# Turned tiles copied from SBUF to SBUF in sixteen pieces, and a DRAM tile of a triangular inverse stored by diagonal blocks

## The chip, the cores and the metric

The kernel runs on one core of one Trainium2 chip. The metric is the device time of one launch in microseconds (us), lower is better. Three runs of the kernel before took 2254.8, 2255.21 and 2257.08 us, so its median is 2255.21 us. One more execution was recorded with the hardware profiler, and every number of a trace in this text comes from it.

## The reference, cut to what matters

The program is one inference step of a decoder with two layers, for a prompt of 1024 tokens and a group of 8 samples of one token each. Both groups go through the same weights; the kernel keeps them side by side as 1032 columns. Each layer projects its normalised input with one large matrix, runs two kinds of recurrent heads, gates the result and projects it back:

```python
h = _rms(x, norm_w[layer]) * (1.0 + scale) + shift
proj = (h @ w_in).astype(f32)          # q, k, v, gates, z of all heads
...                                    # recurrent heads, per layer two kinds
x = x + gate * ((y * silu(z)) @ w_out)
```

The even layer has 8 gated-delta heads and 8 mLSTM heads, the odd layer 4 GLA heads and 4 retention heads. The recurrences are computed in chunks of tokens. Two pieces of this matter here. First, every head needs some of its operands (keys, values) with tokens on the rows, while the projections deliver them with features on the rows; so whole tiles have to be turned. Second, a gated-delta head solves a unit lower triangular system per chunk:

```python
A = jnp.where(tri_strict, decay * kk, 0.0) * beta_h[..., :, None]
rhs = beta_h[..., None] * (jnp.moveaxis(vc, 1, 2) - gam * jnp.einsum('bthd,bhde->bhte', kc, S))
U = lax.linalg.triangular_solve(A + eye, rhs, left_side=True, lower=True, unit_diagonal=True)
```

## The kernel before, in words

**Layout.** Activations lie with features on the 128 partitions and 1032 columns: 1024 prompt tokens and 8 samples. Chunks are 128 tokens long, so there are 8 of them (`NC`). A projection of 128 features is 72 matmuls of 128x128 by 128x344: three column ranges, eight blocks of the contraction, and three products each, since fp32 operands are split into a high and a low part (`whi`, `wlo` for the weights). The weights of one projection are one load of 512 KB into one of two `wf` tiles (`load_w`, L886).

**The order of the work.** No instruction is issued as the Python code reaches it. A class `Recorder` (L178) notes each operation with the memory it reads and writes (`touch`, L244), the operations that it therefore depends on, and an estimated cost, and then orders all of them by list scheduling (`forward`, `backward`), each engine's queue for itself. All DMA transfers are issued by one queue, SP. A transfer counts there as 360 ns of SP, a time that depends on its bytes and on the length of its contiguous runs, and a landing latency of 1400 ns, or 2100 ns above 256 KB. For a tile in SBUF the noted region is a range of partitions and a range of columns; for a tile in DRAM it is one range of addresses, from the first to the last that the access touches (`region`, L198). The engines then run the queues strictly in that order, with semaphores for the real dependences. Since PE's order is fixed too, PE stands still when its next matmul is not ready, even when a later one is.

**The even layer** (`even`, L2186) runs the eight gated-delta heads one after the other (`gdn_proj`, `gdn_mix`) and steps the mLSTM heads between them (`MSTEPS`, L35), so that their projections fill PE while a gated-delta head waits on its own chain. The chain of one gated-delta head is: keys from the convolution, turned and squared (`squares`, `kd`), the matrices `N` of all eight chunks, their inverse `Y` (`inverse`), eight chunk steps with the state `S`, and the output. The large tiles of a head (`k2`, `kd`, `N`, `EM`, `Y` and more) exist once, so that the next head waits for most of them. **The odd layer** (L2209) has the same shape with `gla_mix` and `ret_mix`.

**Turning a tile** (`squares`, L1697). VectorE can transpose 32x32 squares in place of their position. One instruction of it (L1702) turns all squares of the 128x1024 tile and writes them into `y` so that the four squares that belong to one destination partition range lie in one column range. What is left is to carry each 32x256 block from partition group `a`, column group `b` of `y` to partition group `b`, column group `a` of `z`. The kernel before does this through DRAM: one transfer of 512 KB writes `y` to one of four tiles `td` (L1705), and four transfers of 128 KB read it back, one for each group of 32 partitions (L1707). `squares` is called for the keys and values of each gated-delta head (L1199, L1210), for each pair of mLSTM heads (`kwe`, L1426), for the values and the output of each mLSTM head (L1467, L1530) and for the two halves of the values of each GLA and retention head (`v_tokens`, L1715).

**The inverse** (`inverse`, L1279). The 8 matrices of 128x128 have 32 diagonal blocks of 32x32, and each of these two diagonal blocks of 16x16. The 64 small blocks are gathered so that each lies on one partition: four transfers write the 32x32 blocks, one for each position `j` on the diagonal, into a DRAM tile `nd` of 64x528 (L1293), and one transfer reads the 16x16 blocks out of it (L1294). VectorE inverts them in 30 small instructions, the result goes to `yd` in the same way (L1300) and comes back in four reads (L1303). Larger blocks follow with matmuls. Row `m` of `nd` belongs to chunk `c`, position `j` and half `q` as `m = (c, j, q)`, the chunk outermost (L1284).

Of the kernel before, what the change touches and what calls it, by code (L numbers as in the profile page):

```python
# [9 lines left out]
F32 = mybir.dt.float32  # L10
# [7 lines left out]
T = 1024  # L18
# [6 lines left out]
NC = T // L  # L25
# [438 lines left out]
class Step:  # L464
# [814 lines left out]
    def inverse(self, N):  # L1279

        V, G, dma = self.nc.vector, self.nc.gpsimd, self.nc.sync.dma_start

        nd, yd = (self.nyd[x][self.turn(x, 2)] for x in ("nd", "yd"))
        by32 = lambda x, j: x.rearrange("(c j q) x -> c j (q x)", c=NC, j=4)[:, j, 0:1024].rearrange(  # L1284
            "c (s t) -> s c t", t=32)
        by16 = lambda x: x[:, 0:512].rearrange("m (r t) -> m r t", t=32)[:, :, 0:16]
        blocks = [slice(32 * j, 32 * j + 32) for j in range(4)]
        t = self.slot("EM", name="inv")
        D, At, qt, Dt = (t[:, 256 * i:256 * i + 256].rearrange("p (c t) -> p c t", c=NC) for i in range(4))
        nb, yb, tb = (t[0:64, 256 * i:256 * i + 256].rearrange("p (r t) -> p r t", t=16) for i in (1, 2, 3))  # L1290
        dma(yb, self.a["i16"].rearrange("p (r t) -> p r t", t=16))
        for j, b in enumerate(blocks):
            dma(by32(nd, j), N[b, :, b])  # L1293
        dma(nb, by16(nd))  # L1294
        for s in range(15):
            n = 15 - s
            V.tensor_tensor(tb[:, 0:s + 1, 0:n], yb[:, 0:s + 1, s:s + 1].to_broadcast([64, s + 1, n]),
                            nb[:, s:s + 1, s + 1:16].to_broadcast([64, s + 1, n]), op=ALU.mult)
            V.tensor_tensor(yb[:, 0:s + 1, s + 1:16], yb[:, 0:s + 1, s + 1:16], tb[:, 0:s + 1, 0:n], op=ALU.subtract)
        dma(by16(yd), yb)  # L1300

        for j, b in enumerate(blocks):
            dma(D[b], by32(yd, j))  # L1303
        V.transpose(Dt, D)
        p = self.ps(None, [128, NC, 32])
        for c in range(NC):
            for j, b in enumerate(blocks):
                self.mm(p[b, c, :], N[b, c, b], Dt[b, c, :], tile_position=(32 * j, 32 * j))
        V.tensor_tensor(At, p, self.imask.unsqueeze(1).to_broadcast([128, NC, 32]), op=ALU.mult)
        p = self.ps(None, [128, NC, 32])  # L1310
        for c in range(NC):
            for j, b in enumerate(blocks):
                self.mm(p[b, c, :], At[b, c, :], D[b, c, :], tile_position=(32 * j, 32 * j))
        V.tensor_tensor(D, D, p, op=ALU.subtract)
        V.transpose(Dt, D)
        Y = self.slot("Y", [128, NC, L], name="Y")
        G.memset(Y, 0.0)
        for b in blocks:
            V.tensor_copy(Y[b, :, b], D[b])

        p = self.ps(None, [128, 2, NC, 32])
        for c in range(NC):
            for i in (0, 2):
                j = i + 1
                bi, bj = slice(32 * i, 32 * i + 32), slice(32 * j, 32 * j + 32)
                self.mm(p[bj, 0, c, :], N[bi, c, bj], Dt[bi, c, :], tile_position=(32 * i, 32 * j))
        for j in (1, 3):
            bj = slice(32 * j, 32 * j + 32)
            self.act(qt[bj], p[bj, 0], AF.Copy, scale=-1.0)
        p2 = self.ps(None, [128, NC, 64])  # L1330
        for c in range(NC):
            for i in (0, 2):
                j = i + 1
                bi, bj = slice(32 * i, 32 * i + 32), slice(32 * j, 32 * j + 32)
                self.mm(p2[bi, c, 0:32], qt[bj, c, :], D[bj, c, :], tile_position=(32 * j, 32 * i))
            self.mm(p2[32:64, c, 0:32], D[32:64, c, :], qt[32:64, c, :], tile_position=(32, 32))
        V.tensor_copy(Y[0:32, :, 32:64], p2[0:32, :, 0:32])
        V.tensor_copy(Y[64:96, :, 96:128], p2[64:96, :, 0:32])

        iy = t[:, 0:512].rearrange("p (c t) -> p c t", c=NC)  # L1340
        Yt = iy[0:64]
        G.memset(Yt[0:32, :, 32:64], 0.0)
        G.tensor_copy(Yt[0:32, :, 0:32], Dt[0:32])
        G.tensor_copy(Yt[32:64, :, 32:64], Dt[32:64])
        V.tensor_copy(Yt[32:64, :, 0:32], p2[32:64, :, 0:32])
        p3 = self.ps(None, [128, NC, 64])
        for c in range(NC):
            self.mm(p3[64:128, c, :], N[0:64, c, 64:128], Yt[:, c, :], tile_position=(0, 64))
        q3 = iy
        self.act(q3[64:128], p3[64:128], AF.Copy, scale=-1.0)  # L1350
        p4 = self.ps(None, [128, NC, 64])
        for c in range(NC):
            self.mm(p4[0:64, c, :], q3[64:128, c, :], Y[64:128, c, 64:128], tile_position=(64, 0))
        V.tensor_copy(Y[0:64, :, 64:128], p4[0:64])
        return Y
# [341 lines left out]
    def squares(self, y, x, z):  # L1697


        dma = self.nc.sync.dma_start  # L1700
        y, z = y[:, 0:T], z[:, 0:T]
        self.nc.vector.transpose(y.rearrange("p (b c j) -> p b c j", b=4, c=NC),  # L1702
                                 x[:, 0:T].rearrange("p (c b i) -> p b c i", b=4, c=NC))
        d = self.td[self.turn("td", 4)]
        dma(d, y)  # L1705
        for b in range(4):
            dma(z[32 * b:32 * b + 32].rearrange("i (a x) -> i a x", a=4),  # L1707
                d.rearrange("(a i) (b x) -> b i a x", a=4, b=4)[b])
        return z.rearrange("p (a c j) -> p c a j", a=4, c=NC)

    def v_tokens(self, v):
# [407 lines left out]
    def build(self):  # L2119
        tc, nc = self.tc, self.nc  # L2120
        with ExitStack() as ctx:
            cp = ctx.enter_context(tc.tile_pool(name="cp", bufs=1))
            psum = ctx.enter_context(tc.tile_pool(name="psum", bufs=1, space=PSUM))
            dr = ctx.enter_context(tc.tile_pool(name="dr", bufs=1, space=DRAM))
            self.big = {}
            for n in NAMES:
                for i in range(TAGS.get(n, 1)):
                    s = Slot(cp, f"s_{n}{i}", [128, SIZES.get(n, W)])
                    self.nc.slots[s.ap.name] = s
                    self.big[n, i] = s.ap  # L2130
            self.wt = {(n, i): cp.tile([128, 1024], F32 if n == "wf" else F32R, name=f"{n}{i}")
                       for n in WBUFS for i in range(WBUFS[n])}
            self.banks = {(n, i): psum.tile([128, 512], F32, name=f"{n}{i}")
                          for n in BANKS for i in range(BANKS[n])}
            self.arena = cp.tile([128, ARENA], F32, name="arena")
            self.base = cp.tile([128, BASE], F32, name="base")
            self.arena_at = {"base": 0, "even": 0, "odd": 0}
            self.xd = dr.tile([2, KT, 128, W], F32, name="xd")
            self.yd = dr.tile([16, 128, W], F32, name="yd")
            self.gd = dr.tile([4, 8, T], F32, name="gd")  # L2140
            self.ed = dr.tile([8, 8, 8], F32, name="ed")
            self.sd = [dr.tile([16, 128], F32, name=f"sd{i}") for i in range(2)]
            self.spd = dr.tile([16, W], F32, name="spd")
            self.rd = [dr.tile([4, QB], F32, name=f"rd{i}") for i in range(2)]
            self.td = [dr.tile([128, T], F32, name=f"td{i}") for i in range(4)]
            self.nyd = {x: [dr.tile([64, 528], F32, name=f"{x}{i}") for i in range(2)] for x in ("nd", "yd")}
            self.program()
            with tc.manual_schedule():
                self.nc.emit()
# [103 lines left out]
```

## Time and profile before

| quantity | value |
|---|---|
| median of three runs | 2255.21 us |
| time of the profiled execution | 2262.98 us |
| its span, first to last instruction | 2261.2 us |
| mean granted TensorE clock | 0.983 of full speed |
| VectorE busy | 1312.8 us (58%) |
| ScalarE busy | 761.4 us (34%) |
| GpSimd busy | 588.4 us (26%) |
| bytes moved by DMA | 290.61 MB, mean 129 GB/s |

How to read the profile: "PE" is TensorE's matmuls, "DVE" is VectorE, "ACT" ScalarE, "POOL" GpSimd, and "SPq" the SP queue that issues the DMAs. Operations are named by their tiles, output first: `s_mp<-td` is a transfer from `td` in DRAM to a tile in the SBUF slot `mp`, `pj<-s_h,whi` a matmul into a PSUM bank `pj`. Nearly all instructions carry line 448, since the recorder emits them there, so tile names tell more than lines. In a row of the timeline, `[8.71 <-DVE arena]` says that the engine stood still for 8.71 us before this row and what it waited for. A row with x4 is four instructions together. The granted clock is the share of full speed that TensorE's clock was given.

The even layer runs from about 140 to 1200 us, with the start of its output projection at the end; the odd layer's heads run from there to about 2040 us.

### The profile page before, as it was taken

What the parts mean: (1) busy time and instruction counts of PE and PEld (TensorE: products, weight loads), DVE (VectorE), ACT (ScalarE), POOL (GpSimd) and SP (SyncE); (2) the same over time, 40 slices, a digit from 0 to 9 for tenths busy, and PEclk for the clock granted to TensorE, in tenths of its full rate; (3) what the DMA queues carried; (4) which work ended last, traced back from release to release, by engine and by line L of the source; (5) the groups of instructions that cost most, each with busy time, mean ns of one, the idle gap of its engine ahead of it and who ended that gap; (6) DMA issues with size and microseconds to landing.
All of it is one profiled execution on the core that took longest, in us unless ns stands there. A gap on an engine that the chain in (4) does not pass through costs nothing.

```text
span 2261.2 us, 42497 instructions
## 1 busy us (share of the span) xinstructions
PE 2184.1 (97%) x17532; PEld 2036.4 (90%) x17532; DVE 1312.8 (58%) x2559; ACT 761.4 (34%) x1374; POOL 588.4 (26%) x409
## 2 busy tenths in 40 slices
PE   6999999999999998998989999999999999999998
PEld 4877877999999988998889999999999999999997
DVE  6775656576565756666553355745754754755322
ACT  4432313242323323232341135234335334334322
POOL 3120212121121311202330032623622622634210
PEclk9999989999999999999999999999999999999999
DMA  9465564625172535527383222254253253365212
GB/s 263 134 190 161 138 190 115 177 78 149 48 189 75 160 99 123 137 77 189 100 253 117 74 80 69 73 153 124 76 157 119 76 162 106 110 192 176 81 59 92
DMA packets 323383, 290.61 MB, mean 129 GB/s; under 512 B 51963, under 2 KB 289013, under 8 KB 323182
## 3 DMA queue, kind: packets, MB, share of 16 engines
q1 hardware_dynamic: 323190, 287.91, 45.2%
q8 instruction: 137, 2.24, 0.4%
q14 instruction: 56, 0.46, 0.1%
HBM read 213.61 MB, written 74.44 MB: 127 GB/s over the span
## 4 chain that ended last, share of the span: by engine, by line
PE 81%; DMA 8%; DVE 6%; ACT 2%; issue 2%; SPq 1%; POOL 0%; POOLq 0%; ACTq 0%; DVEq 0%
PE pj L448 63%; PE A L448 12%; PE B L448 5%; SPq L448 1%; DMA wf<-in_ada_w 1%; DMA s_mp<-td 1%; DVE s_pt L448 1%; DVE wlo L448 1%; DMA s_h<-in_x_prompt 1%; DVE s_tmp L448 1%; DVE arena L448 1%; DMA td<-s_va 1%; DMA s_pt<-yd 0%; DMA td<-s_vs 0%; DMA s_pt<-td 0%
## 5 line engine op out<-in xcount | busy, mean ns | idle before, releaser
L448 PE MATMUL pj<-s_h,whi 128*128 128x344 f32 (+1 forms) x6024 | 1500.0, 328 | 3.7 <-DVE s_h L448 2.6
L448 PEld LDWEIGHTS pj<-s_h,whi 128*128 128x128 f32 (+1 forms) x6024 | 1046.5, 190 | 33.2 <-issue 19.8
L448 PE MATMUL pj<-s_h,wlo 128*128 128x344 f32 (+1 forms) x3024 | 985.2, 326 | 1.0 <-POOL s_h L448 0.6
L448 PEld LDWEIGHTS pj<-s_h,wlo 128*128 128x128 f32 (+1 forms) x3024 | 573.2, 190 | 12.1 <-issue 8.2
L448 ACT ACTIVATE whi<-wf 128x1024 fp32r<-128x1024 f32 (+1 forms) x146 | 152.1, 1042 | 355.1 <-PE pj L448 309.4
L448 DVE TENSOR_TENSOR wlo<-wf,whi 128x1024 fp32r<-128x1024 f32 x112 | 153.3, 1369 | 195.5 <-ACT whi L448 190.9
L448 ACT ACTIVATE s_pt<-pj 128x344 f32<-128x344 f32 (+1 forms) x170 | 76.7, 452 | 237.0 <-PE pj L448 232.4
L448 POOL TENSOR_TENSOR arena<-arena,base 128x8 f32<-128x8 f32 (+5 forms) x38 | 62.2, 1638 | 286.2 <-DVE arena L448 286.2
L448 POOL TENSOR_TENSOR wlo<-wf,whi 128x1024 fp32r<-128x1024 f32 (+1 forms) x32 | 77.4, 2419 | 169.0 <-ACT whi L448 163.5
L448 POOL TENSOR_TENSOR s_tmp<-s_EM 128x512 f32<-128x512 f32 (+1 forms) x60 | 81.3, 1368 | 81.7 <-DVE s_N L448 28.5
L448 DVE SCALAR_TENSOR_TENSOR s_pt<-s_u,base,s_pt 128x1024 f32<-128x1024 f32 x72 | 95.3, 1323 | 0.1
L448 ACT ACTIVATE s_u<-pj 128x344 f32<-128x344 f32 x93 | 41.2, 452 | 136.6 <-PE pj L448 86.8
L448 DVE SCALAR_TENSOR_TENSOR arena<-arena,A 128x128 f32<-128x128 f32 (+1 forms) x84 | 32.8, 390 | 92.5 <-PE A L448 92.4
L448 DVE SCALAR_TENSOR_TENSOR s_zz<-s_pt,pj 128x344 f32<-128x344 f32 x96 | 48.7, 507 | 62.8 <-ACT s_pt L448 62.1
L448 POOL TENSOR_TENSOR s_tmp<-s_tmp,arena 128x1024 f32<-128x1024 f32 (+2 forms) x26 | 45.3, 1747 | 83.2 <-PE B L448 34.2
L448 POOL MEMSET s_u<- 128x3 f32 x24 | 2.5, 102 | 243.4 <-DVE s_pt L448 243.4
L448 POOL TENSOR_TENSOR s_kd<-s_kd,s_vs 128x1032 f32<-128x1032 f32 x8 | 20.0, 2506 | 169.2 <-ACT s_vs L448 169.2
L448 ACT ACTIVATE s_tmp<-s_tmp 128x1024 f32<-128x1024 f32 (+1 forms) x44 | 46.1, 1057 | 35.7 <-POOL s_tmp L448 34.1
L448 DVE TENSOR_TENSOR s_EM<-s_EM 64x15 f32<-64x15 f32 (+7 forms) x240 | 49.9, 208 | 14.2 <-DMA s_EM<-nd 9.0
L448 DVE SCALAR_TENSOR_TENSOR arena<-arena,B 64x130 f32<-64x130 f32 (+1 forms) x84 | 31.2, 372 | 44.4 <-PE B L448 43.6
L448 ACT ACTIVATE arena<-A,arena 128x128 f32<-128x128 f32 x64 | 23.5, 367 | 92.9 <-PE A L448 92.7
L448 ACT ACT_TABLE_LOAD x41 | 52.6, 1283 | 5.1 <-DMA s_h<-in_x_prompt 4.3
(639 smaller groups left out, 3550.4 us busy)
## 6 DMA issues: line engine op xcount, KB each, us to landing
wf<-in_ev_w_in SPq DMA_DIRECT2D x64, 512.0 KB
wf<-in_od_w_in SPq DMA_DIRECT2D x48, 512.0 KB
wf<-in_ada_w SPq DMA_DIRECT2D x32, 512.0 KB
s_tmp<-sd SPq DMA_DIRECT2D x24, 512.0 KB
s_pt<-yd SPq DMA_DIRECT2D x16, 516.0 KB
td<-s_kd SPq DMA_DIRECT2D x16, 512.0 KB
td<-s_vs SPq DMA_DIRECT2D x16, 512.0 KB
s_v<-td SPq DMA_DIRECT2D x64, 128.0 KB
```

The source lines that it names most:

```text
L448: op.fn(*[self.placed(x) for x in op.args], **{k: self.placed(x) for k, x in op.kw.items()})
```

## The change

- In `squares`, the write to `td` and the four reads are gone. In their place 16 transfers copy `y` to `z` directly, each 32 partitions by 256 columns (32 KB), for `a` outermost and `b` inside it. The four DRAM tiles `td` are no longer allocated.
- In `inverse`, the row of `nd` and `yd` becomes `m = (j, c, q)`, the position on the diagonal outermost. So the four writes of `nd` now touch four address ranges that do not overlap, and likewise the four reads of `yd`. The 64 small blocks come in another order over the partitions, and the arithmetic on each is the same.
- The recorder notes other operations and other dependences, so the order of the whole program is computed anew.

```diff
-        by32 = lambda x, j: x.rearrange("(c j q) x -> c j (q x)", c=NC, j=4)[:, j, 0:1024].rearrange(
+        by32 = lambda x, j: x.rearrange("(j c q) x -> j c (q x)", c=NC, j=4)[j, :, 0:1024].rearrange(
             "c (s t) -> s c t", t=32)
...
         self.nc.vector.transpose(y.rearrange("p (b c j) -> p b c j", b=4, c=NC),
                                  x[:, 0:T].rearrange("p (c b i) -> p b c i", b=4, c=NC))
-        d = self.td[self.turn("td", 4)]
-        dma(d, y)
-        for b in range(4):
-            dma(z[32 * b:32 * b + 32].rearrange("i (a x) -> i a x", a=4),
-                d.rearrange("(a i) (b x) -> b i a x", a=4, b=4)[b])
+        for a in range(4):
+            for b in range(4):
+                dma(z[32 * b:32 * b + 32, 256 * a:256 * a + 256], y[32 * a:32 * a + 32, 256 * b:256 * b + 256])
         return z.rearrange("p (a c j) -> p c a j", a=4, c=NC)
...
-            self.td = [dr.tile([128, T], F32, name=f"td{i}") for i in range(4)]
```

## The prediction, made before the changed kernel had run

> **What bounds the kernel now.** I read the summary of engines first, then the stages, then who PE waits for, then the transfers that end those waits.
>
> ```profile
> PE 2184.1 (97%) x17532; PEld 2036.4 (90%) x17532; DVE 1312.8 (58%) x2559; ACT 761.4 (34%) x1374; POOL 588.4 (26%) x409
> ```
>
> PE is busy for 97% of the span of 2261.2 us, so the change can only win what PE loses: time in which it stands still, and time in which its clock is reduced. The stages (from, to, length, then the busy time of PE, PEld, DVE, ACT and POOL, the granted clock, the DMA share and GB/s) show where it loses:
>
> ```profile
> 140.00:500.00 360.00, 347.11 (x2744) 294.39 (x2745) 223.96 (x524) 104.53 (x206) 66.71 (x51) 0.97 0.55 147
> 500.00:800.00 300.00, 296.93 (x2404) 283.90 (x2404) 195.05 (x456) 89.54 (x179) 59.72 (x47) 0.99 0.49 130
> 800.00:1200.00 400.00, 373.13 (x3056) 351.82 (x3056) 239.79 (x521) 126.30 (x256) 89.10 (x61) 0.97 0.53 138
> 1200.00:2040.00 840.00, 838.06 (x7103) 804.96 (x7103) 474.23 (x712) 307.33 (x481) 290.61 (x175) 1.00 0.38 112
> ```
>
> In the odd layer's heads (last row) PE stands still for 1.9 us of 840 at full clock: nothing can be won there. In the even layer it is idle for 12.9 + 3.1 + 26.9 = 42.8 us, and the missing clock, 0.03 x 360 + 0.01 x 300 + 0.03 x 400, is worth another 25.8 us. So 69 us is the ceiling of any gain, and 39 of them lie between 800 and 1200 us. Who PE waits for, in 140 to 800 and then in 800 to 1200 us:
>
> ```profile
> PE pj L448 <- DMA wf<-in_ada_w: 10.3, 3, 4.3
> ```
> ```profile
> PE A L448 <- DVE arena L448: 8.7, 1, 8.7
> PE B L448 <- ACT s_va L448: 5.5, 1, 5.5
> ```
>
> The first is late loads. I followed the other two back; both end at a turned tile. The first (SP's issues, then the rows of DVE and PE):
>
> ```profile
> 882.58 0.38 SPq L448 DMA_DIRECT2D td<-s_va  x1
> ...
> 886.24 9.03 SPq L448 DMA_DIRECT2D s_mp<-td  x4
> ```
> ```profile
> 902.42 0.48 DVE L448 SCALAR_TENSOR_TENSOR s_zz<-s_mp,base,s_zz 128x256 f32<-128x256 f32 x1 [10.16 <-DMA s_mp<-td]
> ```
> ```profile
> 905.06 0.38 PE L448 MATMUL A<-base,arena 128*8 128x128 f32 x1 [8.71 <-DVE arena L448]
> ```
>
> DVE stood 10.16 us before a gating instruction that reads a turned tile, and the small instructions that PE wanted were queued behind it. Here the tile took 902.42 - 882.58 = 19.84 us from the write's issue to its first reader. The second:
>
> ```profile
> 1053.81 0.81 SPq L448 DMA_DIRECT2D td<-s_va  x1
> 1059.52 1.12 SPq L448 DMA_DIRECT2D s_qs<-gd  x2
> 1060.74 1.95 SPq L448 DMA_DIRECT2D s_pt<-td  x4
> ```
> ```profile
> 1066.85 1.06 ACT L448 ACTIVATE s_va<-s_pt 128x1024 f32<-128x1024 f32 x1 [5.72 <-DVE s_EM L448]
> ```
>
> This one took 13.04 us. ACT's releaser is given as DVE, but ACT reads `s_pt`, which those four transfers fill.
>
> **The change part by part: SP's time.** The rows of issues (shortest, median, longest ns) count the sets, and the last one is the nearest to a piece of 32 rows, since it has 24 rows per transfer:
>
> ```profile
> L448 SPq DMA_DIRECT2D td<-s_kd x16: 319/354/969, 124.6 to 2018.9; - x16
> L448 SPq DMA_DIRECT2D td<-s_vs x16: 326/343/799, 128.5 to 2017.1; - x16
> L448 SPq DMA_DIRECT2D s_qs<-td x16: 313/432/1682, 158.8 to 1052.9; - x16
> L448 SPq DMA_DIRECT2D td<-s_va x16: 319/338/1459, 172.8 to 1175.7; - x16
> L448 SPq DMA_DIRECT2D td<-s_kwe x4: 333/483/1326, 154.9 to 1043.1; - x4
> ```
> ```profile
> L448 SPq DMA_DIRECT2D arena<-in_state_gdn_conv x24: 303/328/1403, 46.8 to 994.3; - x24
> ```
>
> That is 16 + 16 + 16 + 4 = 52 sets: by the code 36 in the even layer and 16 in the odd. Each goes from 5 transfers to 16, 572 more in all. A set that met no traffic, and the landing of the last of four reads elsewhere in the chain of waits:
>
> ```profile
> 860.79 0.36 SPq L448 DMA_DIRECT2D td<-s_kd  x1
> 863.49 1.76 SPq L448 DMA_DIRECT2D s_N<-td  x4
> ```
> ```profile
> 1122.60 3.18 DMA s_pt<-td
> ```
>
> Four issues in a row take 1.76 us, 0.44 each. A new piece costs between 0.33 (the row with 24 rows) and 0.44; I take 0.37, near the former because it is nearer in rows. A set then holds SP for 16 x 0.37 = 5.9 us instead of 0.36 + 1.76 = 2.1, so 3.8 more: 137 us over the even layer's 1060, 61 over the odd layer's 840. SP has that time, since it mostly waits. What is behind it in the queue is delayed by those 3.8 us: weight loads above all. Two weight tiles are in turn, and a projection's 72 matmuls take at least 8.5 us (the odd stage has 838.06 us for 7103 matmuls, 0.118 each, most of them shorter ones), so a load that is ordered early enough hides it; where that cover is gone, a late load costs what one does above, 10.3 / 3 = 3.4 us, and with the lost clock in the proportion of the stages (25.8 to 42.8) 5.5 us.
>
> **The time from turning to use.** Before, in the quiet set: 863.49 - 860.79 = 2.70 us for the write, 3 x 0.44 = 1.32 to the last read, 3.18 for its landing: 7.2 us. After: 15 x 0.37 = 5.55 to the last piece, and its landing. No transfer from SBUF to SBUF is in the trace. Its landing is bounded by the 3.18 above from one side and from the other by the smallest transfer of the chain, of a few rows:
>
> ```profile
> 257.22 1.66 DMA rd<-s_Y
> ```
>
> I take 2.4 us, the middle, as the piece lies between the two in bytes: 8.0 us, so a quiet set gets 0.8 slower (bounds 0 and +1.5). With traffic it turns: the write's landing, which SP had to wait for before it could issue a read, was 1060.74 - 1053.81 = 6.9 us in the second case. After, 5.55 plus a landing as slow as then (1066.85 less the last issue at 1060.74 + 3 x 0.5, so 4.6) is 10.2 instead of 13.0: 2.9 us won. In the first case 5.55 + 7.6 (902.42 less 894.8, the last issue) = 13.1 instead of 19.8, 6.7 won; or nothing, if the stall inside the issue (9.03 us for four) meets the pieces too. PE's two gaps are 8.71 and 5.50 us, so up to 9.6 of these 14.2 us go, with clock in proportion 15. I take 8, since the stall inside the issue may return; bounds 0 and 15. What is late next at both places is the weight split and the reads behind the same transfers, so the gap doesn't close.
>
> The Trainium skill, "DMA: Bandwidth & Descriptors", section "Rules for kernel authors", speaks against the change: many small transfers should be joined into one, because under 64 KB one pays mostly overhead. Paid one after the other, sixteen landings of 2.4 us would be 38 us a set, 43 us more at the two places together, and the kernel would take near 2300 us (an estimate, from that page's rule and the rows here). By the rows above the overheads overlap: four reads are issued in 1.76 us while one landing takes 3.18. So the rule enters below, with the rivals.
>
> **The inverse.** The four writes of `nd` overlap in their address ranges before, so the recorder lets each wait for the one before, and puts other work between; on the chip they need not. Two heads show both cases:
>
> ```profile
> 514.80 1.82 SPq L448 DMA_DIRECT2D nd<-s_N  x4
> 525.52 0.40 SPq L448 DMA_DIRECT2D wf<-in_ev_w_in  x1
> 526.10 0.63 SPq L448 DMA_DIRECT2D s_EM<-nd  x1
> ```
> ```profile
> 766.11 0.33 SPq L448 DMA_DIRECT2D nd<-s_N  x1
> ...
> 789.54 0.65 SPq L448 DMA_DIRECT2D s_EM<-nd  x1
> ```
>
> Together, they take 11.3 us from the first write to the read back; spread, 23.4. After the change the ranges are apart and they can go together in each head, so up to 12 us leave the chain of a head; the read back of `yd` had no such order to lose. PE has other work beside this chain in most heads (between 500 and 800 us it is idle for 3.1 us of 300). What can be won is a part of the rest of the idle time, 26.9 - 14.2 = 12.7 us late and 12.9 early. I take a quarter, 6 us; bounds 0 and 16.
>
> **The sum.** -8 (turned tiles) - 6 (inverse) + 2 (weight loads: less than one late load of 3.4 us net, as each issue is in the recorder's plan) = -12 us. The upper bound of the last term is one late load for each of 8 heads, 44 us. The odd layer adds 0: its sets have the same cost, and full projections cover them. The profiled execution took 2262.98 us, 7.8 above the median of 2255.21; taking -12 from both gives a span near 2249 and a median of 2243 us.
>
> **The rivals.** *Slower: SP as the bound of the weight loads.* SP issues in order, and it also waits for landings that have nothing to do with the transfer in hand:
>
> ```profile
> SPq L448 <- DMA td<-s_va: 7.2, 6, 2.2
> SPq L448 <- DMA td<-s_kd: 7.0, 4, 2.5
> SPq L448 <- DMA wf<-in_ev_w_in: 7.0, 6, 2.7
> ```
>
> No transfer reads a `wf` tile, so the last row is a limit on transfers in flight. Sixteen pieces in a row run into it behind every load that is still under way, and the next load is behind them. For it: 36 sets in 1060 us, with DMA half busy. Against it: SP no longer waits for the landings in the first two rows, and the weight tiles are double. It decides when more than 14 / 5.5, so three, loads come late; with five the sum is -14 + 27 = +13, 2268 us. Chance 0.28. The rule of the Trainium skill on small transfers, named above, would bite here; of the 0.28 it has 0.03, since the rows show overheads that overlap. *No change, within 0.2% (4.5 us, about what a measurement of this kernel can tell):* the new order has its own gaps and gives back what the two known gaps held; 2255 us. For it: two waits make a third of the idle time, and such waits are chance meetings of traffic. Chance 0.17. *Faster by much:* sets and inverse come so early that the late stage's 39 us go nearly all, about -35, 2220 us. Against it: the early loads of `ada_w` and half of the clock stay. Chance 0.12.
>
> **How the numbers follow.** My forecast, faster by some 5 to 25 us, has 0.43; likeliest time 2243. Faster by over 0.2%: 0.43 + 0.12 = 0.55; same 0.17; slower 0.28. The forecast's own range is 2230 to 2250. The 80% range must take in most of the slow case and part of the large gain: 2222 to 2270.
>
> **What would show it.** Right: no `td` rows; a `s_mp<-s_va` group of 16 issues near 0.37 us each; four `nd` writes together in each head, with some 11 us to the read back; PE idle between 800 and 1200 us down from 26.9 to about 15, the odd layer as it is. Wrong: PE waits on `wf` or `whi` in the even layer that weren't there, SP waits on landings of pieces that exceed the `td` rows, or idle time in the odd layer.

## The result, and the profile after

The changed kernel takes 2429.62 us (median of 4 runs, 2427.14 to 2432.0) against 2255.75 us for the kernel before in the same session: a ratio of 1.0768, interval 1.0751 to 1.0785. It is 174 us slower, where 12 us faster was forecast. One execution of an experiment below (pieces counted at 635 ns) took 3471.27 us; it is in that experiment's median and not in its ratio. The profiled execution of the changed kernel has a span of 2425.1 us at a mean granted clock of 0.961 (before 0.983). The summary of engines of the changed kernel:

```profile
PE 2219.9 (92%) x17532; PEld 2061.3 (85%) x17532; DVE 1293.4 (53%) x2559; ACT 758.0 (31%) x1374; POOL 582.3 (24%) x409
```

The number of matmuls is the same. PE is busy for 35.8 us more at the lower clock, and idle for 205.2 us instead of 77.1, so 128.1 us more: together the 163.9 us by which the span grew. The stages (columns as before; by 1200 us the changed kernel is behind, so the last window still holds the end of the even layer and not yet the end of the odd one):

```profile
140.00:500.00 360.00, 323.04 (x2535) 267.09 (x2535) 192.81 (x484) 91.22 (x182) 57.28 (x46) 0.95 0.45 122
500.00:800.00 300.00, 268.71 (x2140) 254.32 (x2139) 170.66 (x389) 80.24 (x166) 50.49 (x40) 0.95 0.34 89
800.00:1200.00 400.00, 342.09 (x2608) 324.74 (x2606) 221.93 (x515) 104.88 (x207) 65.46 (x51) 0.92 0.37 95
1200.00:2040.00 840.00, 810.03 (x6665) 771.82 (x6663) 439.31 (x711) 285.01 (x472) 257.39 (x158) 0.99 0.35 103
```

No stage is spared: PE is idle for 37.0, 31.3, 57.9 and 30.0 us, where it was 12.9, 3.1, 26.9 and 1.9. Of the 30.0 us, 8.9 lie before 1330 us, in the even layer. Every other engine is less busy as well, and so are the DMA engines: everything waits. Who PE waits for in the changed kernel (us in total, times, longest):

```profile
PE B L448 <- ACT s_va L448: 31.0, 3, 18.3
PE pj L448 <- DMA wf<-in_ada_w: 28.5, 7, 9.7
PE pj L448 <- DVE s_zz L448: 17.9, 7, 6.9
PE A L448 <- DVE s_q L448: 13.6, 3, 6.1
PE B L448 <- POOL s_va L448: 13.4, 2, 9.0
```

The waits are many and of many kinds, with the readers of turned tiles (`s_va`, `s_zz`) ahead. GpSimd, the engine in front of PE in the last row, stands behind the pieces itself. It sets columns of `s_va`, the tile that the pieces read, and may do so only when the last of them has read it; before, one write to `td` had to read it, and GpSimd's waits for that were 40.2 us in 3. Now they are:

```profile
POOL s_va L448 <- DMA s_pt<-s_va: 165.3, 8, 40.4
```

The issues of the pieces, one tile at a time (shortest, median, longest ns):

```profile
L448 SPq DMA_DIRECT2D s_pt<-s_va x128: 507/589/1528, 188.0 to 1252.5; - x128
...
L448 SPq DMA_DIRECT2D s_mp<-s_va x128: 508/589/1430, 242.3 to 1314.7; - x128
```

The prediction counted 370 ns, with 330 and 440 as bounds. The shortest of these 256 pieces holds SP for 507 ns, the median one for 589.

The largest of PE's waits, 18.26 us, shows what that does. SP's queue ahead of it, then the three engines behind it:

```profile
857.90 4.31 SPq L448 DMA_DIRECT2D s_v<-s_vs  x7
862.25 0.65 SPq L448 DMA_DIRECT2D s_EM<-nd  x1
862.95 3.83 SPq L448 DMA_DIRECT2D s_v<-s_vs  x6
866.88 0.53 SPq L448 DMA_DIRECT2D wf<-in_ev_w_in  x1
867.51 10.96 SPq L448 DMA_DIRECT2D s_qs<-s_kwe  x16
...
883.70 1.99 SPq L448 DMA_DIRECT2D s_pt<-s_va  x3
885.73 0.65 SPq L448 DMA_DIRECT2D yd<-s_EM  x1
886.42 8.27 SPq L448 DMA_DIRECT2D s_pt<-s_va  x13
```
```profile
868.25 1.23 DVE L448 TENSOR_TENSOR s_vs<-s_v,arena 128x1024 f32<-128x1024 f32 x1 [3.19 <-DMA s_v<-s_vs]
879.93 0.69 DVE L448 TENSOR_TENSOR s_kwe<-s_qs,arena 128x512 f32<-128x512 f32 x1 [4.16 <-DMA s_qs<-s_kwe]
...
881.52 1.22 DVE L448 STREAM_TRANSPOSE s_va<-s_pt 128x1024 f32<-128x1024 f32 x1
```
```profile
896.30 1.06 ACT L448 ACTIVATE s_va<-s_pt 128x1024 f32<-128x1024 f32 x1 [19.60 <-DMA s_pt<-s_va]
```
```profile
897.46 0.77 PE L448 MATMUL B<-s_va,s_mp 128*128 128x130 f32 x2 [18.26 <-ACT s_va L448]
```

Thirteen pieces take 8.27 us, so one leaves every 0.636 us, and sixteen take 10.2. Three sets stand in a row on SP. DVE waits for the first, then for the second, and only then turns the third tile (881.52); that one's pieces are the last thing before ACT and PE. The landing is short: ACT starts 1.61 us after the last issue has ended (886.42 + 8.27 = 894.69), some 2.2 us after that issue began. The inverse's transfers of this kernel, in two heads:

```profile
567.51 1.86 SPq L448 DMA_DIRECT2D nd<-s_N  x4
571.82 0.66 SPq L448 DMA_DIRECT2D s_EM<-nd  x1
...
702.07 2.14 SPq L448 DMA_DIRECT2D nd<-s_N  x4
706.83 0.65 SPq L448 DMA_DIRECT2D s_EM<-nd  x1
```

All four writes leave together, and the read back is issued 4.3 and 4.8 us after the first (3.2 to 8.5 us over the eight heads, where it was 11.3 to 23.4). That the writes go together came as forecast, and the read back is sooner than the 11 us of the forecast.

### The profile page after: what moved, and what is told of

The parts are those of the page before. It is cut to its first block, busy times and chain, and to the rows that moved or that the text cites. A ratio compares the mean times of both kernels' runs of the same rounds, so it can differ in the third digit from the quotient of the medians.

```text
span 2425.1 us, 43209 instructions
## 1 busy us (share of the span) xinstructions
PE 2219.9 (92%) x17532; PEld 2061.3 (85%) x17532; DVE 1293.4 (53%) x2559; ACT 758.0 (31%) x1374; POOL 582.3 (24%) x409
## 2 busy tenths in 40 slices
DMA packets 325885, 263.44 MB, mean 109 GB/s; under 512 B 61115, under 2 KB 298165, under 8 KB 325678
## 5 line engine op out<-in xcount | busy, mean ns | idle before, releaser
L448 PE MATMUL pj<-s_h,whi 128*128 128x344 f32 (+1 forms) x6024 | 1513.4, 330 | 30.0 <-DVE s_zz L448 17.9
L448 PEld LDWEIGHTS pj<-s_h,whi 128*128 128x128 f32 (+1 forms) x6024 | 1054.1, 191 | 66.6 <-issue 26.1
L448 PE MATMUL pj<-s_h,wlo 128*128 128x344 f32 (+1 forms) x3024 | 988.0, 327 | 1.0 <-POOL s_h L448 0.6
L448 PEld LDWEIGHTS pj<-s_h,wlo 128*128 128x128 f32 (+1 forms) x3024 | 577.3, 191 | 13.4 <-issue 9.9
L448 ACT ACTIVATE whi<-wf 128x1024 fp32r<-128x1024 f32 (+1 forms) x146 | 152.1, 1042 | 358.5 <-PE pj L448 311.4
L448 DVE TENSOR_TENSOR wlo<-wf,whi 128x1024 fp32r<-128x1024 f32 x112 | 143.3, 1280 | 222.2 <-ACT whi L448 205.0
L448 ACT ACTIVATE s_pt<-pj 128x344 f32<-128x344 f32 (+1 forms) x170 | 76.2, 451 | 219.8 <-PE pj L448 204.9
L448 POOL TENSOR_TENSOR arena<-arena,base 128x8 f32<-128x8 f32 (+5 forms) x38 | 62.2, 1641 | 282.0 <-DVE arena L448 280.6
L448 POOL TENSOR_TENSOR wlo<-wf,whi 128x1024 fp32r<-128x1024 f32 (+1 forms) x32 | 78.1, 2442 | 173.5 <-ACT whi L448 169.4
L448 POOL TENSOR_TENSOR s_tmp<-s_EM 128x512 f32<-128x512 f32 (+1 forms) x60 | 83.0, 1398 | 102.8 <-DVE s_N L448 35.6
L448 DVE SCALAR_TENSOR_TENSOR s_zz<-s_pt,pj 128x344 f32<-128x344 f32 x96 | 48.7, 508 | 93.8 <-ACT s_pt L448 93.6
L448 DVE SCALAR_TENSOR_TENSOR s_pt<-s_u,base,s_pt 128x1024 f32<-128x1024 f32 x72 | 97.4, 1353 | 0.5
L448 DVE SCALAR_TENSOR_TENSOR arena<-arena,A 128x128 f32<-128x128 f32 (+1 forms) x84 | 32.8, 391 | 100.4 <-PE A L448 97.9
L448 ACT ACTIVATE s_u<-pj 128x344 f32<-128x344 f32 x93 | 41.4, 452 | 140.4 <-PE pj L448 85.4
L448 POOL MEMSET s_u<- 128x3 f32 x24 | 2.4, 102 | 291.9 <-DVE s_pt L448 291.9
L448 PE MATMUL pj<-wf,base 128*32 128x512 f32 x128 | 44.4, 658 | 28.5 <-DMA wf<-in_ada_w 28.5
L448 DVE TENSOR_TENSOR s_EM<-s_EM 64x15 f32<-64x15 f32 (+7 forms) x240 | 50.7, 211 | 25.8 <-DMA s_EM<-nd 18.2
L448 POOL TENSOR_TENSOR s_tmp<-s_tmp,arena 128x1024 f32<-128x1024 f32 (+2 forms) x26 | 45.4, 1754 | 66.8 <-PE A L448 42.9
L448 POOL TENSOR_TENSOR s_kd<-s_kd,s_vs 128x1032 f32<-128x1032 f32 x8 | 19.5, 2434 | 165.2 <-ACT s_vs L448 165.2
L448 PE MATMUL B<-s_va,s_mp 128*128 128x130 f32 x128 | 28.8, 318 | 30.8 <-ACT s_va L448 20.4
L448 ACT ACTIVATE arena<-A,arena 128x128 f32<-128x128 f32 x64 | 23.4, 366 | 100.5 <-PE A L448 100.4
```

The costliest lines, as they stand in the source:

```text
L448: op.fn(*[self.placed(x) for x in op.args], **{k: self.placed(x) for k, x in op.kw.items()})
```

## The experiments

Every ratio below is to the kernel before, run on the same chip in the same session. The recorder's constant of 360 ns for a transfer's time on SP matters from the third run on: it enters both passes of the list scheduling (L320, L413) and nothing else. It changes the order of the queues, not what is computed or moved.

**One part at a time.** First the inverse alone: L1284 as in the change, `squares` as before.

> The diagonal-block order alone, with turned tiles by DRAM as before. Price theory (each piece holds SP for 0.59 us plus a gap, so a set of sixteen takes some 10 us where I had 5.9): the whole loss is in the pieces, so this is not slower than before: 2240 to 2258 us. Inverse theory (the new order of nd and yd gives a bad order of the whole program): 2300 us or more.

Measured: 2258.28 us, ratio 1.0025 (1.0008 to 1.0042). The four writes are together, and yet nothing is won:

```profile
657.10 1.78 SPq L448 DMA_DIRECT2D nd<-s_N  x4
661.85 0.63 SPq L448 DMA_DIRECT2D s_EM<-nd  x1
```

Then the sixteen pieces alone, L1284 as before.

> The sixteen pieces alone, nd and yd ordered by chunks as before. Price theory: the loss of the full change or a little more, 2400 to 2460 us. Inverse theory: near 2256 us.

Measured: 2426.37 us, ratio 1.078 (1.0744 to 1.0816). The whole loss is in the pieces.

**The order or the price.** The pieces take more of SP's time than the four reads did, and the order of the queues was made with 360 ns for each. These are two causes. If the pieces' time itself is the cost, it stays wherever they stand. If it is the order, another order without another transfer takes the loss away. The full change, with the pieces counted at what they take:

```diff
+        op.hold = 635.0 if queue == "sync" and all(self.in_sbuf(x) for x in writes + reads) else 360.0
...
-            occupied[i] = op.cost if q == "tensor" else max(360.0, op.size / op.rate) if q == "sync" else (
+            occupied[i] = op.cost if q == "tensor" else max(op.hold, op.size / op.rate) if q == "sync" else (
...
-                free[q] = t + 360.0
+                free[q] = t + op.hold
```

> The full change, but the recorder counts 635 ns of SP for a transfer from SBUF to SBUF instead of 360, so that it orders the program by the cost that the trace shows. Price theory, in the form that SP's time is simply in the chain of each head: little is won back, 2380 us or more. Order theory (the loss comes from an order that was made for pieces of 360 ns): most is won back, under 2320 us.

Measured: 2304.28 us, ratio 1.0226 (1.0194 to 1.0258). The same 832 pieces, 125 us less. The order decides most of the loss, and 51 us remain, though the count now agrees with the trace. The next run counts more than they take: 900 for 635 in the first line of that diff.

> The full change, with 900 ns of SP counted for a transfer from SBUF to SBUF, more than the 635 ns that one holds it by the trace. With 360 the kernel took 2430 us, with 635 2304. Order theory (PE's fixed order is made for tiles that come earlier than they do, and PE stands still by the difference): an order with slack does as well or better, 2265 to 2305 us. Price theory (what is left is SP's time itself): no better than 2300, likely 2310 to 2340, as the order is now wrong on the other side.

Measured: 2244.84 us, ratio 0.9964 (0.9946 to 0.9982), faster than the kernel before and below what either theory expected. The stages of this run, and its pieces (lines added to the recorder make L448 into L453):

```profile
140.00:500.00 360.00, 348.81 (x2817) 298.38 (x2816) 227.15 (x527) 107.30 (x206) 68.17 (x54) 0.99 0.50 138
500.00:800.00 300.00, 297.21 (x2558) 283.16 (x2557) 201.66 (x481) 89.63 (x178) 59.30 (x46) 1.00 0.38 103
800.00:1200.00 400.00, 387.84 (x3043) 367.59 (x3042) 246.57 (x515) 130.67 (x265) 90.44 (x60) 1.00 0.47 131
```

```profile
L453 SPq DMA_DIRECT2D s_pt<-s_va x128: 507/589/1497, 181.5 to 1112.5; - x128
```

A piece holds SP as long as ever, and PE's idle time of 57.9 us late in the even layer is 12.2 us. So the time of the pieces on SP is hidden in this order, which leaves room for it: the price theory falls. More room still, 1200:

> The full change, with 1200 ns counted for each transfer from SBUF to SBUF where 900 were counted (0.36 in the change as made). The same pieces, other places in the order. Order theory (the loss is the distance between the time that the order allows a set on SP and the time that it takes): the room is enough at 900, so more room wins nothing, and sets placed further ahead push other transfers of SP back: 2240 to 2320 us, at or above the 2244.84 of 900. Price theory (the pieces' own time on SP costs, wherever they stand): 2380 or more, as in the change as made. Below 2235 us would say that room was still missing at 900.

Measured: 2326.73 us, ratio 1.0328 (1.0307 to 1.0349), just over the expected range. More room isn't always better: of the four counts, 900 is the best. The pieces are the same at 900 and at 1200, and yet 3.6% lie between the two; why is open.

**The count of small transfers, or their kind.** One write to `td` and sixteen reads of 32 KB from it, with the inverse by diagonals and 360 ns for each transfer:

```diff
-        for b in range(4):
-            dma(z[32 * b:32 * b + 32].rearrange("i (a x) -> i a x", a=4),
-                d.rearrange("(a i) (b x) -> b i a x", a=4, b=4)[b])
+        for a in range(4):
+            for b in range(4):
+                dma(z[32 * b:32 * b + 32, 256 * a:256 * a + 256], d[32 * a:32 * a + 32, 256 * b:256 * b + 256])
```

> By DRAM with one write as before, but read back in sixteen pieces of 32 KB instead of four of 128 KB; diagonal-block order kept. So SP issues one transfer more per set than the change does, and none from SBUF to SBUF. Price theory, in the form that the kind of transfer is what costs: a piece from DRAM holds SP for some 0.33 us, a set is 5.6 us of SP, and the kernel lands between 2260 and 2330 us. Count theory (any sixteen transfers in a row cost this, by the limit on transfers in flight): issues near 0.6 us each, or waits of SP for their landings, and 2400 us or more.

Measured: 2359.6 us, ratio 1.0484 (1.0447 to 1.052), between the two expectations. One of its reads, the same 32 rows of 1 KB as a piece:

```profile
L448 SPq DMA_DIRECT2D s_pt<-td x128: 302/419/1491, 190.8 to 1215.5; - x128
```

It holds SP for 419 ns, 170 less than a piece from SBUF: the kind costs, beside the number. Sixteen in a row hold it for longer than that median says, 0.46 to 0.62 us each in these two sets:

```profile
527.02 7.28 SPq L448 DMA_DIRECT2D s_N<-td  x16
...
588.91 9.91 SPq L448 DMA_DIRECT2D s_pt<-td  x16
```

With the write that is 7.6 to 10.4 us a set, where 17 x 0.36 = 6.1 are counted; the loss of 107 us is in line with that distance. It was still open whether the number of transfers costs by itself, so the same kernel ran with 700 ns for these reads:

> The turned tiles by DRAM with one write and 16 reads of 32 KB each, blocks ordered by diagonals, as in the run with 16 reads, and now 700 ns counted for each of these reads where 360 were. Order theory: the loss of that run (2359.6 against 2252.9) mostly goes: 2245 to 2290 us. Count theory (many small transfers cost by their number, through the queue's rings or the DMA engines): it stays, 2330 to 2370 us.

Measured: 2238.0 us, ratio 0.9928 (0.9908 to 0.9948), below the expected range. The loss is gone with the transfers unchanged, so the count theory falls.

**The reverse.** If the order is what matters, the kernel before can be made slow with its own order. The write stays in the recorder's books but issues nothing, and each of the four reads issues four pieces from SBUF: five transfers are counted, 1.8 us in the pass that makes the order (`forward`), where 10.2 pass.

```diff
-        dma(d, y)
+        issue = self.nc.sync.eng.dma_start
+
+        def four(out, src, whole):
+            for a in range(4):
+                issue(out[:, a, :], whole[32 * a:32 * a + 32])
+
+        self.nc.add("sync", "dma_start", lambda out, src: None, (d, y), {})
         for b in range(4):
-            dma(z[32 * b:32 * b + 32].rearrange("i (a x) -> i a x", a=4),
-                d.rearrange("(a i) (b x) -> b i a x", a=4, b=4)[b])
+            self.nc.add("sync", "dma_start", four, (z[32 * b:32 * b + 32].rearrange("i (a x) -> i a x", a=4),
+                        d.rearrange("(a i) (b x) -> b i a x", a=4, b=4)[b]), dict(whole=y[:, 256 * b:256 * b + 256]))
```

> The pieces in the order that was made for the path by DRAM: the recorder still sees one write and four reads, but the write issues nothing and each read issues its four pieces from SBUF instead (one dependence is added, so that the first tile isn't overwritten before the last piece). nd is ordered by chunks as before. SP's time and its pieces are those of the full change, the order of all engines is the one of before. Order theory: the order allows a set some 8 us and it takes some 12, as loaded sets do before, so the loss is a fraction, 2280 to 2350 us. Price theory (SP's time by itself): the loss of the full change, 2400 us or more.

Measured: 2494.19 us, ratio 1.1063 (1.1026 to 1.11). The expectation of the order theory missed: it took the old order for a good one. By the same theory it had to be worse than the change, since the distance is 8.4 us a set here and 4.4 there, and it was; but that was seen only afterwards. The time lies where the price theory had put it, so this run by itself doesn't decide between the two. The runs at 635, 900 and 700 do.

**Whether more room helps by itself.** The kernel before with 450 ns for every transfer, in both places where 360 stands:

> The kernel before with nothing changed but the recorder's count of SP for every transfer, 450 ns instead of 360; four reads in a row took 0.44 us each in its trace. Order theory: the order gets closer to what the chip does, same or a little faster, 2235 to 2258 us. Price theory says nothing of it: 2255 us.

Measured: 2255.22 us, ratio 1.0015 (0.9996 to 1.0033): no change. The kernel before with 2500 ns more for the landing of the transfers of `td`:

```diff
+        op.slack = 2500.0 if queue == "sync" and any(x.name.startswith("td") for x in reads + writes) else 0.0
...
-                end = dma + (2100.0 if op.size > 1 << 18 else 1400.0)
+                end = dma + (2100.0 if op.size > 1 << 18 else 1400.0) + op.slack
```

> The kernel before, with 2500 ns more counted for the landing of the turned tiles' transfers by DRAM; nothing that is computed or moved changes, only the order. If the gain of the change with 900 counted comes from the order alone (more room ahead of the turned tiles, whatever carries them), this gains as well: 2235 to 2250 us. If it comes from the path that the change shortens, this stays where the kernel before is, 2250 to 2260 us.

Measured: 2272.8 us, ratio 1.0072 (1.0046 to 1.0099), above both expectations. Room alone isn't the gain.

**Which part gains once there is room.** Three runs fill a table of the two parts. The old path with 2800 ns for each of its four reads, so 11.2 us a set as in the sixteen reads at 700, and the diagonal order:

> The turned tiles by DRAM with one write and four reads, as in the kernel before, the inverse ordered by diagonals, and 2800 ns of SP counted for each of the four reads: the same 11.2 us a set that the run with 16 reads at 700 ns counted, without its small transfers. Order theory (the 0.7% gained with 16 reads or 12 pieces comes from the room that the order leaves a set, whatever carries it): 2230 to 2248 us. Path theory (it comes from smaller pieces, which reach their readers with less waiting): 2250 to 2262, as in the run with the diagonal order alone.

Measured: 2241.93 us, ratio 0.9957 (0.994 to 0.9975), as the order theory had it. The pieces at 900 with the inverse in its old order:

> The sixteen pieces from SBUF to SBUF with 900 ns counted for each, and the inverse's DRAM tile in its old order, with the chunk outermost: the run at 900 without the second part of the change. If the diagonal order is worth something once the pieces have room (the prediction's 6 us), this takes 2248 to 2256 us; if it is worth nothing, as it was alone, 2240 to 2248, the 2244.84 of the run with both.

Measured: 2262.14 us, ratio 1.0055 (1.0035 to 1.0075), above both ranges. And the old path with 2800 and the old order:

> The kernel before with nothing changed but the order: 2800 ns of SP counted for each of the four reads of a turned tile. Order theory: 2230 to 2248 us, a gain without either part of the change. Path theory: 2250 to 2260, no gain. Above 2270: room that the transfers don't use costs, as it did with 2500 ns more counted for their landing (2272.8).

Measured: 2268.75 us, ratio 1.0079 (1.0064 to 1.0095), a loss where the order theory expected a gain and nearly the loss of the run with more landing. The ratios side by side:

| turned tiles | inverse by chunks | inverse by diagonals |
|---|---|---|
| by DRAM, 360 ns counted | 1 | 1.0025 |
| sixteen pieces, 360 | 1.078 | 1.0768 |
| by DRAM, four reads at 2800 | 1.0079 | 0.9957 |
| by DRAM, sixteen reads at 700 | | 0.9928 |
| sixteen pieces, 900 | 1.0055 | 0.9964 |

With room for the turned tiles, the two orders with the inverse by diagonals are faster than those by chunks, by 0.9% with the pieces and 1.2% by DRAM, some 20 to 27 us. PE's idle time between 140 and 1200 us goes with it: 26.1 us against 36.8 with the pieces, and 22.5 against 41.4 by DRAM. The way by which a tile is turned is worth next to nothing: 0.9957, 0.9928 and 0.9964. The transfers of the inverse differ as follows, first in the pieces at 900 with the old order, then in the pieces at 900 by diagonals:

```profile
664.79 0.53 SPq L453 DMA_DIRECT2D nd<-s_N  x1
667.10 0.58 SPq L453 DMA_DIRECT2D nd<-s_N  x1
671.09 0.42 SPq L453 DMA_DIRECT2D nd<-s_N  x1
674.00 0.58 SPq L453 DMA_DIRECT2D nd<-s_N  x1
675.88 0.66 SPq L453 DMA_DIRECT2D s_EM<-nd  x1
```
```profile
645.52 1.80 SPq L453 DMA_DIRECT2D nd<-s_N  x4
648.76 0.65 SPq L453 DMA_DIRECT2D s_EM<-nd  x1
```

11.1 us from the first write to the read back, against 3.2; over the eight heads 7.3 to 12.5 against 3.1 to 8.7. But each entry of the table is one order, and orders that differ only in what was counted differ without a cause that was found by 0.8% (1 and 1.0079) in the kernel before and by 3.6% (0.9964 and 1.0328) with the pieces. The 0.9 and 1.2% have the same sign twice and are no larger than such differences, so a gain from the diagonal order is likely and not shown.

**Fewer pieces.** A quarter of the pieces stays on its own partitions (`a` equal to `b`), and there an engine can copy it inside SBUF. In both runs GpSimd does that, and twelve pieces stay:

```diff
+            p, c = slice(32 * a, 32 * a + 32), slice(256 * a, 256 * a + 256)
+            self.nc.gpsimd.tensor_copy(z[p, c], y[p, c])
             for b in range(4):
-                dma(z[32 * b:32 * b + 32, 256 * a:256 * a + 256], y[32 * a:32 * a + 32, 256 * b:256 * b + 256])
+                if a != b:
+                    dma(z[32 * b:32 * b + 32, c], y[p, 256 * b:256 * b + 256])
```

With 635 ns counted:

> The full change with the 635 ns count, but only twelve transfers a set: the four blocks that stay in their partition range are copied by GpSimd. SP holds 7.6 us a set instead of 10.2. Price theory, for what is left of the loss at 2304 us (51 us for 8.1 us more SP time a set): 51 x 5.5 / 8.1 = 35 us, so 2290 us. Order theory: the rest has other causes, so 2300 us or more, as GpSimd gets 208 more instructions.

Measured: 2259.66 us, ratio 1.0035 (1.0013 to 1.0057), against 1.0226 with sixteen: better than either theory expected. So part of the 51 us that were left at 635 went with the four pieces, by a way that neither theory names and that wasn't followed. GpSimd's copies are cheap:

```profile
L453 POOL COPY s_pt<-s_va x32: 388/398/1383, 168.4 to 1120.5; 32x256 f32<-32x256 f32 x32
```

With 900 ns counted:

> The full change with the four diagonal blocks of a turned tile copied by GpSimd inside SBUF and only the other twelve moved by transfers, and 900 ns counted for each of these. Order theory: with room for them, four pieces fewer a set leave SP some 2.5 us a set (4 x 0.635) that nothing waits for: 2235 to 2250 us, near or just below the 2244.84 of sixteen pieces at 900. Price theory: a quarter of the pieces' cost goes, from 2429.6 to some 2385 us. A rival: GpSimd's copies end later than the pieces that they replace and hold up the product after them: 2255 to 2290.

Measured: 2235.38 us, ratio 0.9926 (0.9904 to 0.9947), the fastest of all, level with the sixteen reads at 700. It beats both kernels.

## Why the prediction was wrong

**The step that failed: "each issue is in the recorder's plan".** With that, the prediction priced the delay on SP at +2 us. Each issue is in the plan, but at 360 ns. A piece takes 0.636, so sixteen take 4.4 us more than the order allows, in each of 52 sets. SP's queue is fixed and so are all others; what was placed behind a set, on any engine, comes late, and the next set stands behind the last one, as ahead of the wait of 18.26 us. The prediction saw that SP had idle time to spare and took that for cover. SP has it still: its waits add up to some 1490 us of 2425, where they were 1790 of 2261. But idle time in a queue of fixed order is only cover where the order has put it, ahead of the reader. The sum of all terms, -12 us, measured +174; the runs at 635 and 900 show it as a matter of order, since the pieces are the same and the loss goes to 51 us and then to nothing. The distance between count and time isn't the whole account: at 635 it is about nothing and 51 us stay, and that rest is open.

**The price of a piece.** 0.37 us was taken from loads with 24 rows from DRAM, the row nearest in the number of rows; 0.44, from four reads of `td` with 32 partitions, was the upper bound. Reads from DRAM of a piece's exact shape measure 0.419 one by one, within that bound, and 0.46 to 0.62 in the two rows of sixteen above, beyond it. What no row of before showed is the kind: SBUF to SBUF holds SP 0.170 us longer. The bound should have reached beyond the rows for a kind of transfer that the trace doesn't have. A set takes 10.2 us of SP, not 5.9. At 0.37 a piece, the 0.36 that the order counts would have been nearly right, so the failed step rests on this price.

**The landing.** The prediction's 2.4 us (1.66 to 3.18), from the start of the last issue, was near the mark. The readers of the three sets ahead of the largest wait start 2.1, 2.1 and 2.2 us after it. Two pieces in the chain that ended last, both in the odd layer, took longer, one of them beyond the bound (start and length in us):

```profile
1909.44 3.75 DMA s_v<-s_vs
2007.28 3.11 DMA s_v<-s_vs
```

**The turned tiles, -8 us.** Not shown by any run. In the change as made the sets came later. With room, path against path the ratios lie between 0.9928 and 0.9964 by diagonals, and the four reads by DRAM are in the middle. The gaps of the kernel before at these tiles were a matter of its order: PE's 6.0 us behind ScalarE's `s_va` are in none of the runs that count 700 ns or more, by pieces or by DRAM. One reading under this term was also wrong. The 6.9 us of the second tile aren't the landing of its write: for 4.1 of them SP stood behind VectorE (`s_EM`) with another transfer, ahead of the reads, and it had no wait for `td<-s_va` there.

**The inverse, -6 us.** The mechanism was right and showed in each run by diagonals: four writes together in nearly all heads, 3.1 to 10.6 us to the read back, some 5 in the mean, where the kernel before has 17.5. Alone it gave nothing (1.0025). With room the two pairs of orders differ by 20 to 27 us in its favour, which the spread of orders doesn't let stand as shown, and why it should take room elsewhere wasn't followed.

**The rivals.** The slower rival had the right engine, SP, and the wrong mechanism and size. It looked for weight loads late behind a limit on transfers in flight; that its row shows such a limit was argued, and no run tests it. Its row fell from 7.0 us in 6 waits:

```profile
SPq L448 <- DMA wf<-in_ev_w_in: 3.3, 5, 0.8
```

SP's waits for all loads of `wf` together hardly moved, 38.9 us before and 37.8 after. PE's waits for late loads did come as the sign of being wrong had it: 7 where there were 3, 28.5 us where there were 10.3, all before 500 us. So the rival's point of decision, three late loads, was passed; but these are 18.2 us of the 128.1 by which PE's idle time grew, and between 500 and 2040 us no load is late. The Trainium skill's rule ("DMA: Bandwidth & Descriptors", section "Rules for kernel authors"), that transfers under 64 KB pay mostly overhead, had the right sign for the change as made. But where the order has room, sixteen reads of 32 KB (0.9928) are no slower than four of 128 KB (0.9957). So here the overhead of a small transfer is seen in its time on the issuing queue, and an order with room hides that.

**The odd layer, 0.** It lost as well: 22.1 us of idle time between 1330 and 2190 us, where its 840 us had 1.9 before. Its full projections didn't cover the sets in this order.

## What to carry to other kernels

In a program whose queues run in an order made beforehand, the question about an added instruction isn't only what it costs but what the order believes it costs: look up the constant, and multiply the difference by the count. That gives the size and no more: here 4.4 us in 52 sets are 229 us, and 174 were lost. Mend the estimate before judging the change, and try more than one value. At the 635 ns of the trace 1.0768 became 1.0226, and only at 900 did it become 0.9964; at 1200 it was 1.0328. With such a spread between orders, a difference of 1% between two of them says little about the part of the change that was meant.

## What the runs showed of the hardware

- A transfer of 32 rows of 1 KB held SP for 589 ns (median; shortest 507) from SBUF to SBUF, and for 419 ns (shortest 302) from DRAM to SBUF. A read of 128 KB on 32 partitions had 432 ns before, and a write of 512 KB from SBUF to DRAM 338 to 354 ns in the three large groups. So the size hardly mattered, and of the three kinds SBUF to SBUF held SP longest.
- Thirteen pieces in a row left every 0.636 us, 0.047 more than the median issue; sixteen in a row took 10.96 us, 0.685 each.
- The reader of a set of pieces started 2.1 to 2.2 us after the last issue began, in three sets.
- GpSimd copied 32 x 256 f32 inside SBUF in 398 ns, less than the 0.636 us that the same block takes of SP.
- All transfers together moved 263.44 MB instead of 290.61, 27 MB less, and that won nothing.
